# Half of the output products of both branches by seven instead of eight, with their operands made beside the gate units

## The chip, the cores and the metric

One core of a Trainium2 chip runs the kernel. The metric is device time in microseconds (us). The kernel before takes 2490.22 us, the median of three runs from 2490.2 to 2490.33.

## The reference, cut to what matters

Two layers (`DEPTH = 2`) act on 640 tokens of 1024 features: 512 frames of new streams and 8 x 16 frames of running ones. Each layer has a feed-forward half, a mixer, and a second feed-forward half. The change lies in the end of the mixer:

```
z  = h @ w_in            # conv B | conv C | conv V | q | k | v | gates
g  = sigmoid(g + b_gate); g_conv, g_attn = split(g)
m  = g_conv * (y_conv @ w_conv_out) + g_attn * (y_attn @ w_attn_out)
x += m @ w_o
```

`y_conv` and `y_attn` have 512 features each; `g_conv`, `g_attn` and `m` have 1024. All of it is float32.

## The kernel before, in words

**Layout.** Features lie on the 128 partitions and the 640 tokens along the free dimension, so 1024 features are eight tiles of 128 x 640. The tokens are cut into halves t1 and t2 of 320. All weights come as one stream `in_wst` of 512 KB pieces (`raw`, three buffers), in the order in which they are used. The function `_stream` lays them out, following `mixer_order`.

**Precision.** A float32 value is split into a high part of type fp32r and a low part, the rest: ScalarE casts `whi<-raw` (L347) and VectorE subtracts `wlo<-raw,whi` (L352). A product is three matmuls: high by high, high by low, low by high. Operands are split in the same way (L234 and L235).

**Slabs.** The weights in their two parts are called a slab here: `whi` and `wlo` of 128 x 1024, three buffers each. `slab()` takes the next slab and prepares the one two places on; `prep` issues the cast, `flush` the subtraction, `ahead` the sums of weights that the next slab needs.

**Products by seven.** Where two tiles of outputs (or of features) and two halves of tokens form a 2 x 2 problem, seven half products take the place of eight, at the price of sums of weights and of operands. The seven kinds of operands are called X11, X21, XN6, XT5, XT7, X22 and XT4. Their weights take two pieces of the stream and make four slabs: the first is piece one as it is; the second needs three sums of 128 x 512 on VectorE (L287, `raw<-raw,raw`, `s<-raw,raw` and a second `raw`), the third needs one more (`raw<-s,raw`), the fourth (half a slab) none. `gate_pair` in `outputs` does one pair of gate tiles so: seven blocks of 12 matmuls of 320 columns (L442), in three PSUM banks `qa`, `qb`, `qc`. Blocks X11 and X21 use the first slab, XN6 and XT5 the second, XT7 and X22 the third, XT4 the fourth. Block XT7 ends in a VectorE sum `g<-qa,c` that has to be done before XT4 may add to the same bank. After the seven blocks VectorE has scaled both gates by the norm (L1495, L1503, L1509), and ScalarE takes the sigmoids (L1330).

**Products as they are.** `out(m, y)` multiplies one 128-column tile of `w_conv_out` or `w_attn_out` ("co" and "ao") by the four tiles of `y_conv` or `y_attn`: 4 x 3 x 2 = 24 matmuls of 320 columns (L418, PSUM tile `py`). VectorE multiplies `py` by the gate (L1526; for "ao" L1528 and a sum into `mm`). Two calls of `out` use one slab.

**Order of the stage.** `outputs` runs gates 2 and 3, then `out` 0 to 3, and from there a gate unit of two gates and two calls of `out` in turn, to gates 14 and 15 and `out` 14 and 15. Gates below 8 belong to the convolution branch, the others to attention. Inside gate unit 2 the four tiles of `y_conv` are split (`take`), inside unit 8 those of `y_attn`. During the last two `out` the sums `mm` are split for `w_o` (`give`), which follows with 8 x 48 matmuls.

**What sets the order.** In `outputs` TensorE, VectorE and ScalarE work strictly in the order in which the code issues instructions (`tc.manual_schedule(engines=ORDERED)`). An instruction that waits holds up everything behind it on its engine.

The lines that set the pace of a gate unit before:

```python
s3 = slab(True)[0]
DVE.tensor_tensor(out=u, in0=u, in1=rr, op=ALU.mult)
sigmoid(u, m)
...
block(pa, s3, 0, XT4, every, False, True)
DVE.tensor_tensor(out=g[:, t1], in0=pa, in1=rr[:, t1], op=ALU.mult)
sigmoid(g, m + 1, -1.0)
flush()
```

Of the kernel before, what the change touches and what calls it, by code (L numbers as in the profile page):

```python
# [55 lines left out]
)  # L56

ROWS = (1, 2)

MARGIN = 2, 4  # L60
LEAN = {"a0": (1, 6), "b0": (1, 5), "a1": (1, 5), "b1": (1, 5)}
# [52 lines left out]
def mixer_order():  # L114

    mix = lambda *rows: ("mix", rows)
    out = [("v", None)] + [mix(("q", p), ("k", p)) for p in range(AW // P)]
    for c in range(0, CT, 2):  # L120
        out += [mix(("C", c + i), ("V", c + i)) for i in range(2)] + [mix(("B", c), ("B", c + 1))]
    gates = [mix(("g", m), ("g", m + 1)) for m in range(0, 2 * KT, 2)]
    out += gates[:2] + [("co", m) for m in range(4)]
    for i, g in enumerate(gates[2:]):
        name, m = ("co", 4 + 2 * i) if i < 2 else ("ao", 2 * i - 4)
        out += [g, (name, m), (name, m + 1)]
    return out + [("o", m) for m in range(KT)]


def kinds():  # L130
# [5 lines left out]
def stages():  # L136

    out, done = [], []

    def end(kind):  # L140
        done.append((kind, out[:]))
        out.clear()

    def plain(n):
        out.extend([8] * (n // 8) + [n % 8] * (n % 8 > 0))

    def ffn(name):
        held = 0
        for what, a in ffn_order(name):
            if what == "gu":  # L150
                plain(held)
                held = 0
                out.append("gu")
            elif what == "std":
                held += 2 * KT
            elif what == "cut":
                plain(held)
                held = 0
            elif what == "rows":
                plain(held)  # L160
                held = 0
                out.append("gu")
            elif what == "ends":
                held += KT * len(a)
            else:
                held += sum(len(js) for _, js in a)
        plain(held)

    for l in range(L):
        ffn(f"a{l}")  # L170
        end("ffn")
        held = 0
        for what, _ in mixer_order():
            if what == "mix":
# [12 lines left out]
def two(ps):  # L187
    return ps[:, :, :HT]
# [7 lines left out]
def trunk(ctx: ExitStack, tc: tile.TileContext, xin, wst, small, pbias, samplebias, kcache, vcache, gfin,  # L196
# [137 lines left out]
    def prep(i):  # L334

        if i < len(ready) or i >= len(slabs):
            return
        assert i == len(ready)
        parts = source(i)
        hi = wp.tile([P, CH], F32R, tag="whi", name=f"whi{i}", bufs=3)  # L340
        lo = wp.tile([P, CH], F32R, tag="wlo", name=f"wlo{i}", bufs=3)
        ready.append((hi, lo))
        o = 0
        for src, c in parts:
            d = slice(o, o + c.stop - c.start)
            o = d.stop
            ACT.copy(hi[:, d], src[:, c])  # L347
            pending.append((lo[:, d], src[:, c], hi[:, d]))

    def flush():  # L350
        for lo, src, hi in pending:
            DVE.tensor_tensor(out=lo, in0=src, in1=hi.bitcast(F32), op=ALU.subtract)  # L352
        pending.clear()
# [82 lines left out]
    def block(ps, s, half, ops, ks, start, stop):  # L436

        for kp in ks:
            w = [z[:, (half * NP + kp) * P : (half * NP + kp + 1) * P] for z in s]
            xh, xl = ops(kp)  # L440
            for j, (a, b) in enumerate(((w[0], xh), (w[0], xl), (w[1], xh))):
                PE.matmul(ps, a, b, start=start and kp == 0 and j == 0,  # L442
                          stop=stop and kp == NP - 1 and j == 2, skip_group_check=True)
# [869 lines left out]
    def mixer(l, after):  # L1313
        with tc.tile_pool(name=f"yp{l}", bufs=1, reuse_waits="tile") as yp, \
# [84 lines left out]
            with tc.tile_pool(name=f"gp{l}", bufs=1, reuse_waits="tile") as gp, \  # L1399
                 tc.manual_schedule(engines=ORDERED):  # L1400
                hold[0] = True
                mo = outputs(l, gp, ops.X, st, cs, ycs, yas, sigmoid, gates)
        ex = after()
        with tc.manual_schedule(engines=ORDERED):
            hold[0] = True
# [56 lines left out]
        def t5(self, kp):  # L1462
            self.parts(*(z[:, HT:] for z in self.h[2 * kp]), self.a[kp][:, 1])

    def outputs(l, gp, X, st, cs, ycs, yas, sigmoid, gates):
# [4 lines left out]
        mm = ycs + [spare[i // 2][:, i % 2] for i in range(CT)]  # L1470
        X11, X21, X22, XN6, XT5, XT7, XT4 = (X[i] for i in ("11", "21", "22", "N6", "T5", "T7", "T4"))
        c1, u2, c5 = cs
        every = range(NP)

        def gate_pair(m, then=None):
            n = f"{l}_{m}"
            pa, pb, pc = (att(f"q{i}{n}")[:, :HT] for i in "abc")
            u, g = gates[m], gates[m + 1] = tmp(f"g{n}"), tmp(f"g{n}_1")
            s0 = quiet()
            block(pa, s0, 0, X11, every, True, True)  # L1480
            ACT.copy(c1, pa)
# [9 lines left out]
            ACT.copy(c5, pc)  # L1491
            s2 = slab(True)[0]
            block(pa, s2, 0, XT7, every, False, True)
            add(g[:, t2], pa, c5)
            DVE.tensor_tensor(out=g[:, t2], in0=g[:, t2], in1=rr[:, t2], op=ALU.mult)  # L1495
# [7 lines left out]
            DVE.tensor_tensor(out=u, in0=u, in1=rr, op=ALU.mult)  # L1503
# [5 lines left out]
            DVE.tensor_tensor(out=g[:, t1], in0=pa, in1=rr[:, t1], op=ALU.mult)  # L1509
            sigmoid(g, m + 1, -1.0)  # L1510
            flush()

        def parts(pool, tag, name, src):
            hi, lo = (pool.tile([P, T], F32R, tag=f"{tag}{i}", name=f"{name}{i}") for i in ("hi", "lo"))
            split(hi, lo, src)
            return hi, lo

        def out(m, y, then=None):

            py = acc(f"py{l}_{m}")  # L1520
            product(py, y)
            if then:
                then()
            g = gates[m]
            if m < KT:
                DVE.tensor_tensor(out=halves(mm[m]), in0=two(py), in1=halves(g), op=ALU.mult)  # L1526
# [5 lines left out]
        yc, ya, mo = [], [], []  # L1532

        def take(y, name, srcs):
# [7 lines left out]
        gate_pair(2, lambda: take(yc, "yc", ycs))  # L1542
        for m in range(4):
            out(m, yc)
        for m in range(4, 2 * KT, 2):
            gate_pair(m, (lambda: take(ya, "ya", [yas[:, c, :] for c in range(CT)])) if m == KT else None)
            y = yc if m < KT else ya
            last = m == 2 * KT - 2
            out(m, y, (lambda: give(range(3))) if last else None)
            out(m + 1, y, (lambda: give(range(3, 6))) if last else None)  # L1550
        give(range(6, KT))
        return mo

# [518 lines left out]
def _stream(i):  # L2072
# [9 lines left out]
    for l in range(L):  # L2082
# [36 lines left out]
        for what, m in mixer_order():  # L2119
            if what == "v":  # L2120
                out.append(v.reshape(KT // 2, 2, P, AW).transpose(0, 2, 1, 3).reshape(-1, P, CH))
            elif what == "mix":
                out.append(chunks(held))
                held = []

                out.append(chunks([rows[name][a][o::2] for name, a in m for o in range(2)]))
            else:
                held.append(rows[what][m])
        out.append(chunks(held))
# [71 lines left out]
```

## Time and profile before

| | |
|---|---|
| median of three runs | 2490.22 us |
| the profiled execution, its own time | 2489.97 us |
| its span, first to last instruction | 2488.2 us |
| TensorE busy, matmuls | 2473.6 us (99%), 17312 matmuls |
| VectorE busy | 2140.2 us (86%) |
| ScalarE busy | 1355.6 us (54%) |
| the stage `outputs`, layer 0 | about 635 to 778 us of the span |
| the same stage, layer 1 | about 1867 to 2010 us of the span |

How to read it: the busy time of an engine is the union of its instructions, so a share of 99% says that the engine has hardly a gap. Matmuls overlap: each is listed with about 309 ns, but the next one starts earlier. The start times in a timeline tell the pace. VectorE's instructions overlap a little as well.

### The profile page before, as it was taken

What the parts mean: (1) busy time and instruction counts of PE and PEld (TensorE: products, weight loads), DVE (VectorE), ACT (ScalarE), POOL (GpSimd) and SP (SyncE); (2) the same over time, 40 slices, a digit from 0 to 9 for tenths busy, and PEclk for the clock granted to TensorE, in tenths of its full rate; (3) what the DMA queues carried; (4) which work ended last, traced back from release to release, by engine and by line L of the source; (5) the groups of instructions that cost most, each with busy time, mean ns of one, the idle gap of its engine ahead of it and who ended that gap; (6) DMA issues with size and microseconds to landing.
All of it is one profiled execution on the core that took longest, in us unless ns stands there. A gap on an engine that the chain in (4) does not pass through costs nothing.

```text
span 2488.2 us, 43913 instructions
## 1 busy us (share of the span) xinstructions
PE 2473.6 (99%) x17312; PEld 2421.3 (97%) x17312; DVE 2140.2 (86%) x3533; ACT 1355.6 (54%) x2151; POOL 295.2 (12%) x449
## 2 busy tenths in 40 slices
PE   9999999999999999999999999999999999999998
PEld 8999999889999999999999999998999999999998
DVE  7999998888777899998799999988886769999997
ACT  6555556665444555555665555566644455555555
POOL 0111112211000001111001011121110000111111
PEclk9999999999999999999999999999999999999999
DMA  4443544335223334445334343453442233444444
GB/s 155 126 118 101 125 117 123 113 106 174 77 85 111 94 102 106 112 117 120 99 92 111 109 117 102 116 128 107 133 157 86 77 111 88 109 115 106 112 117 117
DMA packets 109710, 279.22 MB, mean 112 GB/s; under 512 B 12448, under 2 KB 52000, under 8 KB 109504
## 3 DMA queue, kind: packets, MB, share of 16 engines
q1 hardware_dynamic: 69552, 220.10, 28.2%
q0 software_dynamic: 39520, 56.08, 12.2%
q8 instruction: 135, 2.21, 0.4%
q14 instruction: 71, 0.58, 0.1%
q10 hardware_dynamic: 432, 0.25, 0.0%
HBM read 230.56 MB, written 7.94 MB: 96 GB/s over the span
## 4 chain that ended last, share of the span: by engine, by line
PE 92%; DVE 4%; ACT 2%; issue 1%; DMA 1%; SPq 0%; DVEq 0%; ACTq 0%; POOLq 0%
PE pab L442 12%; PE paa L442 11%; PE pcb L442 6%; PE daa L1120 6%; PE pca L442 5%; PE dab L1120 5%; PE py L418 4%; PE po L418 4%; PE qa L442 4%; PE pbb L442 3%; PE dca L1120 3%; PE pba L442 3%; PE dcb L1120 2%; PE ma_cv L442 2%; PE ma_qk L442 2%; PE pv L1607 2%
## 5 line engine op out<-in xcount | busy, mean ns | idle before, releaser
L352 DVE TENSOR_TENSOR wlo<-raw,whi 128x1024 fp32r<-128x1024 f32 (+1 forms) x569 | 580.0, 1021 | 156.2 <-ACT whi L347 151.8
L347 ACT CAST whi<-raw 128x1024 fp32r<-128x1024 f32 (+1 forms) x569 | 505.2, 891 | 381.8 <-PE pbb L442 47.3
L347 ACT CAST whi<-s 128x1024 fp32r<-128x1024 f32 (+1 forms) x158 | 150.4, 952 | 296.1 <-issue 111.3
L442 PE MATMUL pab<-xhib,whi 128*128 128x320 f32 x704 | 217.7, 309 | 0.0
L442 PE MATMUL pab<-xhib,wlo 128*128 128x320 f32 x704 | 217.3, 309 | 0.0
L442 PE MATMUL pab<-xlob,whi 128*128 128x320 f32 x704 | 217.2, 309 | 0.0
L442 PE MATMUL paa<-xloa,whi 128*128 128x320 f32 x640 | 197.6, 309 | 0.6 <-DVE xloa L679 0.6
L442 PE MATMUL paa<-xhia,whi 128*128 128x320 f32 x640 | 197.9, 309 | 0.2 <-DVE ga L287 0.2
L442 PE MATMUL paa<-xhia,wlo 128*128 128x320 f32 x640 | 197.6, 309 | 0.0
L352 DVE TENSOR_TENSOR wlo<-s,whi 128x1024 fp32r<-128x1024 f32 (+1 forms) x158 | 173.4, 1098 | 4.4 <-ACT whi L347 4.4
L1142 POOL DMA_DIRECT2D x<-c_a x80 | 69.9, 1021 | 574.9 <-ACT ahia L1024 205.6
L442 PEld LDWEIGHTS pab<-xhib,whi 128*128 128x128 f32 x704 | 132.1, 188 | 0.9 <-issue 0.9
L442 PEld LDWEIGHTS pab<-xlob,whi 128*128 128x128 f32 x704 | 132.2, 188 | 0.0
L442 PEld LDWEIGHTS pab<-xhib,wlo 128*128 128x128 f32 x704 | 132.2, 188 | 0.0
L1142 POOL DMA_DIRECT2D x<-c_b x72 | 62.7, 1001 | 582.2 <-ACT ahib L1024 205.8
L442 PEld LDWEIGHTS paa<-xhia,whi 128*128 128x128 f32 x640 | 120.1, 188 | 1.3 <-DVE ga L287 0.5
L442 PEld LDWEIGHTS paa<-xloa,whi 128*128 128x128 f32 x640 | 120.2, 188 | 1.1 <-DVE xloa L679 1.1
L442 PEld LDWEIGHTS paa<-xhia,wlo 128*128 128x128 f32 x640 | 120.2, 188 | 0.2
L442 PE MATMUL pcb<-xhib,wlo 128*128 128x320 f32 x352 | 108.8, 309 | 0.0
L442 PE MATMUL pcb<-xlob,whi 128*128 128x320 f32 x352 | 108.6, 309 | 0.0
L442 PE MATMUL pcb<-xhib,whi 128*128 128x320 f32 x352 | 108.6, 309 | 0.0
L287 DVE TENSOR_TENSOR raw<-s,raw 128x512 f32<-128x512 f32 x158 | 107.9, 683 | 0.0
(757 smaller groups left out, 8072.4 us busy)
## 6 DMA issues: line engine op xcount, KB each, us to landing
raw<-in_wst SPq DMA_DIRECT2D x375, 512.0 KB, 3.6
x<-c_a POOLq DMA_DIRECT2D x80, 160.0 KB, 4.6
x<-c_b POOLq DMA_DIRECT2D x72, 160.0 KB, 3.6
lent<-in_wst POOLq DMA_DIRECT2D x34, 256.0 KB, 3.9
kc<-in_kcache SPq DMA_DIRECT2D x32, 256.0 KB, 4.8
vc<-in_vcache SPq DMA_DIRECT2D x16, 512.0 KB, 4.7
x<-u_a POOLq DMA_DIRECT2D x40, 160.0 KB, 4.0
x<-u_b POOLq DMA_DIRECT2D x36, 160.0 KB, 4.0
```

The costliest lines, as they stand in the source:

```text
L287: DVE.tensor_tensor(out=out, in0=a, in1=b, op=op)
L347: ACT.copy(hi[:, d], src[:, c])
L352: DVE.tensor_tensor(out=lo, in0=src, in1=hi.bitcast(F32), op=ALU.subtract)
L418: PE.matmul(ps[:, a, :HT], w, x[a] if isinstance(x, tuple) else x[:, a * HT : (a + 1) * HT], start=first and j == 0 and not seeded, stop=l ...
L442: PE.matmul(ps, a, b, start=start and kp == 0 and j == 0, stop=stop and kp == NP - 1 and j == 2, skip_group_check=True)
L1120: PE.matmul(ps[u], w, y, start=start and i == 0 and j == 0, stop=i == 1 and j == 2, skip_group_check=True)
L1142: POOL.dma_start(x[ms[2 * u + r]][:, cols], z[:, u], accum_op=ALU.add)
L1607: PE.matmul(pv[t], xx[:, t * P : (t + 1) * P], w[:, kk * AW : (kk + 1) * AW], start=c == 0 and kk == 0 and j == 0, stop=c == KT // 2 - 1 a ...
```

## The change

- **Seven for eight.** Output tiles 4 to 7 of the convolution branch and 2 to 5 of the attention branch no longer go through `out`. A new unit `rows` makes four tiles together: seven blocks of 12 matmuls of 320 columns, in PSUM tiles A, B (of the pool of `py`) and two banks `rc` (of the pool of `qa`). The weights of the four tiles come in the layout for seven products and make four slabs with four sums, as those of a gate unit do.
- **Operands.** XT5, XT7, XT4 and XN6 of `y` are made in place from each pair of its tiles (`mixed`): four VectorE instructions of 320 columns, a ScalarE cast of 1280 columns and a VectorE subtraction of 1280 columns. The three steps stand at three places of a gate unit: behind the first slab's flush, behind the copy of block XT5, and behind `ahead` of block XT7. Gate units 4, 6, 10 and 12 each carry one pair. X11, X21 and X22 are parts of the tiles that `take` split already.
- **Order.** Gates 2, `out` 0 to 3, gates 4, gates 6, `rows` of "co", gates 8, `out` 8 and 9, gates 10, gates 12, `rows` of "ao", gates 14, `out` 14 and 15. The products of `rows` "ao" are multiplied into the gates and added to `mm` in gate unit 14 (`total`).
- **Sigmoids.** They are collected in `lates` and issued behind the next unit's first ScalarE copy, or at the head of the next `out`.
- **Buffers.** The first four tiles of `mm` lie in new memory, the last four where `y_conv` lay.

The core of the diff:

```diff
+SEVEN = {"co": (4, 5, 6, 7), "ao": (2, 3, 4, 5)}
...
-        def gate_pair(m, then=None):
+        def gate_pair(m, at):
...
             ACT.copy(c1, pa)
+            due()
             prep(used[0] + 1)
             flush()
+            at[0]()
             block(pb, s0, 1, X21, every, True, True)
...
             ACT.copy(c5, pc)
+            at[1]()
             s2 = slab(True)[0]
...
             flush()
             ahead()
-            if then:
-                then()
+            at[2]()
             block(pc, s2, 1, X22, every, False, True)
...
-            sigmoid(u, m)
+            lates.append(lambda: sigmoid(u, m))
...
-            sigmoid(g, m + 1, -1.0)
+            lates.append(lambda: sigmoid(g, m + 1, -1.0))
...
+        def mixed(z):
+            z = z.rearrange("p c (a b) -> p (c a) b", a=2)
+            e1, e2, o1, o2 = (z[:, i] for i in range(4))
+            add(e1, e1, e2, ALU.subtract)
+            add(e2, o2, e2, ALU.subtract)
+            for out, a in ((o2, e1), (o1, o2)):
+                DVE.scalar_tensor_tensor(out=out, in0=a, scalar=-1.0, in1=out, op0=ALU.mult, op1=ALU.subtract)
+            yield
+            i = len(more) % 2
+            hi, lo = (gp.tile([P, 4, HT], F32R, tag=f"x{i}{p}", name=f"x{p}{l}_{len(more)}") for p in ("hi", "lo"))
+            ACT.copy(hi, z)
+            more.append((hi, lo))
+            yield
+            DVE.tensor_tensor(out=lo, in0=z, in1=hi.bitcast(F32), op=ALU.subtract)
+            yield
...
+            w = quiet()
+            mul(a, w, 0, X11, True)
+            ACT.copy(s1, two(A))
+            due()
+            prep(used[0] + 1)
+            flush()
+            mul(b, w, 1, X21, True)
+            add(s1, two(B), s1)
+            w = slab(True)[0]
+            flush()
+            mul(a, w, 0, XN6, False)
+            ACT.copy(s2, two(A))
+            gated(0, [s1[:, u] for u in range(2)], t1)
+            mul(c, w, 1, XT5, True)
+            for u in range(2):
+                ACT.copy(s5[:, u], c[u])
+            w = slab(True)[0]
+            mul(a, w, 0, XT7, False)
+            add(s5, two(A), s5)
+            flush()
+            ahead()
+            gated(1, [s5[:, u] for u in range(2)], t2, -1.0)
+            mul(c, w, 1, X22, False)
+            for u in range(2):
+                add(s2[:, u], c[u], s2[:, u])
+            w = slab(True)[0]
+            gated(0, [s2[:, u] for u in range(2)], t2)
+            mul(a, w, 0, XT4, False)
+            flush()
+            gated(1, a, t1, -1.0)
...
+        beside(4, ycp[0])
+        beside(6, ycp[1])
+        rows("co", yc)
+        gate_pair(8, [none, none, lambda: take(ya, "ya", [yas[:, c, :] for c in range(CT)])])
+        out(8, ya)
+        out(9, ya)
+        beside(10, yas[:, 0:2])
+        beside(12, yas[:, 2:4])
+        rows("ao", ya)
+        gate_pair(14, [lambda: total(0), none, lambda: (total(1), give(range(1)))])
+        out(14, ya, lambda: give(range(1, 4)))
+        out(15, ya, lambda: give(range(4, 6)))
```

`gated` multiplies a staged sum or a PSUM tile by two gates, 320 columns at a time; `beside(m, z)` is gate unit m with the three steps of `mixed(z)`.

More of the change, by code (lines that the diff above doesn't have):

```diff
@@ L122, in mixer_order @@
     gates = [mix(("g", m), ("g", m + 1)) for m in range(0, 2 * KT, 2)]
[L123 to L127, printed above, removed]
+    out += gates[:2] + [("co", m) for m in range(4)] + gates[2:4] + [("rows", ("co", SEVEN["co"]))]
+    out += [gates[4], ("ao", 0), ("ao", 1), gates[5], gates[6], ("rows", ("ao", SEVEN["ao"]))]
+    return out + [gates[7], ("ao", 6), ("ao", 7)] + [("o", m) for m in range(KT)]
 def kinds():
@@ L173, in stages @@
         for what, _ in mixer_order():
-            if what == "mix":
+            if what in ("mix", "rows"):
                 plain(held)
@@ L1401, in mixer @@
                 hold[0] = True
-                mo = outputs(l, gp, ops.X, st, cs, ycs, yas, sigmoid, gates)
+                mo = outputs(l, gp, ops.X, st, cs, ycp, yas, sigmoid, gates)
         ex = after()
@@ L1463, in t5, with outputs @@
             self.parts(*(z[:, HT:] for z in self.h[2 * kp]), self.a[kp][:, 1])
-    def outputs(l, gp, X, st, cs, ycs, yas, sigmoid, gates):
+    def outputs(l, gp, X, st, cs, ycp, yas, sigmoid, gates):
         rr, t1, t2 = st.rr, slice(0, HT), slice(HT, T)
         spare = [gp.tile([P, 2, T], F32, name=f"mm{l}_{i}") for i in range(2)]
-        mm = ycs + [spare[i // 2][:, i % 2] for i in range(CT)]
+        ycs = [z[:, i] for z in ycp for i in range(2)]
+        mm = [spare[i // 2][:, i % 2] for i in range(CT)] + ycs
+        stage = [halves(st.caps)] + [gp.tile([P, 2, HT], F32, name=f"rs{l}_{i}") for i in range(2)]
         X11, X21, X22, XN6, XT5, XT7, XT4 = (X[i] for i in ("11", "21", "22", "N6", "T5", "T7", "T4"))
@@ L1473, in outputs, with due @@
         every = range(NP)
-        def gate_pair(m, then=None):
+        lates = []
+        def due():
+            for f in lates:
+                f()
+            lates.clear()
+        def gate_pair(m, at):
             n = f"{l}_{m}"
@@ L1532, in outputs @@
         yc, ya, mo = [], [], []
+        more = []
         def take(y, name, srcs):
@@ L1540, in give @@
                 mo.append(parts(hp, "h", f"m{l}_{m}", mm[m]))
-        gate_pair(2, lambda: take(yc, "yc", ycs))
+        def mixed(z):
[13 more added lines that the diff above has]
+            yield
@@ L1543, in outputs, with total, beside @@
+        def total(r):
+            for m in SEVEN["ao"][2 * r : 2 * r + 2]:
+                add(mm[m], mm[m], gates[KT + m])
+        def beside(m, z):
+            z = mixed(z)
+            gate_pair(m, [lambda: next(z)] * 3)
+        none = lambda: None
+        gate_pair(2, [none, none, lambda: take(yc, "yc", ycs)])
         for m in range(4):
             out(m, yc)
[L1545 to L1550, printed above, removed]
+        beside(4, ycp[0])
@@ L2126, in _stream @@
                 out.append(chunks([rows[name][a][o::2] for name, a in m for o in range(2)]))
+            elif what == "rows":
+                out.append(chunks(held))
+                held = []
+                name, ms = m
+                out.append(chunks([rows[name][a][o::2] for r in range(2) for o in range(2)
+                                   for a in ms[2 * r : 2 * r + 2]]))
             else:
```

33 lines of the change are left out of this document (added).

## Prediction

> **What bounds the kernel now.** I read the page first, then the waits of TensorE, the chain that ended last, and then one gate unit instruction by instruction on VectorE and ScalarE.
>
> ```profile
> span 2488.2 us, 43913 instructions
> PE 2473.6 (99%) x17312; PEld 2421.3 (97%) x17312; DVE 2140.2 (86%) x3533; ACT 1355.6 (54%) x2151; POOL 295.2 (12%) x449
> ...
> PE poa L418 <- ACT whi L735: 5.4, 1, 5.4
> PE paa L442 <- DVE xloa L679: 0.6, 1, 0.6
> PE po L418 <- DVE m_6lo L235: 0.4, 2, 0.2
> ...
> 674.17 7.04 PE py L418 x48
> 693.51 7.04 PE py L418 x48
> ```
>
> TensorE is the bound. It waits 5.4 us once, at the start, and its other waits are below 1 us each. So a matmul less is time saved, and every wait that TensorE gets is time lost. The last two rows give the pace: 48 matmuls of two calls of `out` take 7.04 us, 0.1467 us each. Between them lie 693.51 - 674.17 - 7.04 = 12.30 us, one gate unit of 84 matmuls. One block of 12 takes 1.76 us. VectorE at 86% is next; whether it can follow is the question.
>
> ```profile
> 681.99 0.68 DVE L287 TENSOR_TENSOR raw<-s,raw 128x512 f32<-128x512 f32 x1
> 684.41 1.22 DVE L352 TENSOR_TENSOR wlo<-raw,whi 128x1024 fp32r<-128x1024 f32 x1 [1.75 <-ACT whi L347]
> 685.56 0.48 DVE L287 TENSOR_TENSOR g<-qb,capsm 128x320 f32<-128x320 f32 x1
> 685.96 0.68 DVE L352 TENSOR_TENSOR wlo<-raw,whi 128x512 fp32r<-128x512 f32 x1
> 690.10 0.49 DVE L287 TENSOR_TENSOR g<-qa,c 128x320 f32<-128x320 f32 x1 [3.46 <-PE qa L442]
> 690.63 0.49 DVE L1495 TENSOR_TENSOR g<-g,rrm 128x320 f32<-128x320 f32 x1
> 691.04 1.22 DVE L352 TENSOR_TENSOR wlo<-raw,whi 128x1024 fp32r<-128x1024 f32 x1
> 692.17 0.48 DVE L287 TENSOR_TENSOR g<-qc,capsm 128x320 f32<-128x320 f32 x1
> 692.69 0.83 DVE L1503 TENSOR_TENSOR g<-g,rrm 128x640 f32<-128x640 f32 x1
> 693.55 0.49 DVE L1509 TENSOR_TENSOR g<-qa,rrm 128x320 f32<-128x320 f32 x1
> 693.95 1.22 DVE L352 TENSOR_TENSOR wlo<-raw,whi 128x1024 fp32r<-128x1024 f32 x1
> 695.20 0.69 DVE L287 TENSOR_TENSOR raw<-raw,raw 128x512 f32<-128x512 f32 x1
> 695.93 0.69 DVE L287 TENSOR_TENSOR s<-raw,raw 128x512 f32<-128x512 f32 x1
> 696.54 0.69 DVE L287 TENSOR_TENSOR raw<-raw 128x512 f32<-128x512 f32 x1
> 697.14 0.82 DVE L1526 TENSOR_TENSOR mm<-py,g 128x640 f32<-128x640 f32 x1
> 697.88 0.68 DVE L352 TENSOR_TENSOR wlo<-s,whi 128x512 fp32r<-128x512 f32 x1
> ...
> 683.00 0.43 ACT L1481 COPY capsm<-qa 128x320 f32<-128x320 f32 x1 [4.46 <-PE qa L442]
> 683.32 1.06 ACT L347 CAST whi<-raw 128x1024 fp32r<-128x1024 f32 x1
> 684.67 0.62 ACT L347 CAST whi<-raw 128x512 fp32r<-128x512 f32 x1 [0.29 <-PE qb L442]
> 688.27 0.43 ACT L1491 COPY c<-qc 128x320 f32<-128x320 f32 x1 [1.33 <-PE qc L442]
> 693.55 1.55 ACT L1330 ACTIVATE g<-g,sm 128x640 f32<-128x640 f32 x2 [0.86 <-DVE g L1503]
> ...
> 681.04 0.31 PE L442 MATMUL qa<-hhim,whi 128*128 128x320 f32 x1
> ```
>
> This is gate unit 6, which starts at 681.04. In the first column the starts of neighbours give what VectorE really spends on one instruction: 0.40 us for 320 columns (685.56 to 685.96), 0.60 for 512 (697.88 to its other half), 0.74 for 640 (697.14 to 697.88), 1.14 for 1024 (684.41 to 685.56), so 1.40 for 1280 by the same slope. One that needs the result of the one before starts 0.13 later (690.10 to 690.63 is 0.53; 695.20 to 695.93 is 0.73). VectorE idles 1.75 and 3.46 us here: in a gate unit it has room. But note where: it waits for block XT7 (690.10 is 9.05 us into the unit), and nearly all its work comes after that. The sums for the next unit (695.20 on) fall under the calls of `out`, with 7.04 us for them.
>
> **What the change takes from TensorE.** A group of four tiles falls from 4 x 24 = 96 matmuls to 84. There are two groups in a layer and two layers: 48 matmuls x 0.1467 = **7.04 us less**. The columns are 320 as before and `rows` has the blocks of a gate unit, so I keep the pace.
>
> **What it adds to VectorE and ScalarE.** Of the built program I read the order on each engine, which is fixed in this stage. A gate unit costs VectorE: slabs 1.14 + 1.20 + 1.14 + 0.60, sums 4 x 0.60 + 0.12, gates 5 x 0.40 + 0.74 + 2 x 0.13; together 9.6 us. A step of `mixed` adds 4 x 0.40 + 3 x 0.13 = 2.0 and a subtraction of 1.40: **13.0 us against 12.32 us of TensorE**. The scalar_tensor_tensor in it costs as much as a plain one:
>
> ```profile
> L1079 DVE SCALAR_TENSOR_TENSOR doa<-doa 128x320 f32<-128x320 f32 x18 | 8.7, 484 | 0.0
> raw<-in_wst SPq DMA_DIRECT2D x375, 512.0 KB, 3.6
> ```
>
> `rows` costs 6.6 for slabs and their sums, 2 x 0.74 for the sums over two tiles, 10 x 0.40 + 0.13 for the rest: 12.2 us. So gates 4, gates 6 and `rows` ask 38.2 us of VectorE in 36.96 us of TensorE, with no `out` between them. ScalarE gets a cast of 1280 columns, 1.25 us by the slope of its rows; with slabs 3.6, three copies 1.2 and sigmoids 1.55 it is at 7.6 of 12.3 us, and only its place in the chains counts.
>
> **The walk.** Time 0 is the start of gate unit 4; VectorE has caught up there, as in the rows (681.99 comes 0.95 us into the unit).
> - *Gates 4.* The third slab is split at 3.36 to 4.58, as before. `mixed` runs 4.50 to 6.5, the sum on `qb` and the fourth slab end at 7.5. All this fits before XT7 (9.05). After it: 9.05 sum, 9.58 scale, 9.98 next slab, 11.12 three weight sums, 13.05 subtraction of 1280, 14.45 sum on `qc`, 14.98, 15.72, and at 16.12 the first half of the second slab of gates 6, done at 16.80. TensorE needs it in gates 6 at 12.32 + 3.52 + 0.30 = 16.14: **0.7 us lost**.
> - *Gates 6.* The sum for the third slab ends at 18.0, behind all that; ScalarE has the two sigmoids done at 17.4, casts to 19.1, VectorE subtracts to 20.34, just in time for 20.38. That idle 1.2 us of VectorE is not made good: `mixed` to 22.3, then 0.4 and 0.6. The sum on XT7 ends at 23.75, where XT4 could start at 23.60: **0.15 lost**. The cast of 1280 (price 1.25) stands before the cast of the next slab, which ends at 24.6. The chain of gates 4 from there gives the second slab of `rows` at 31.44; TensorE needs it at 29.4: **2.1 lost**.
> - *`rows`.* Third slab at 34.99 for 35.0. Two sums, eight products and the next weight sums: second slab of gates 8 at 44.1 for 43.8, the third at 48.4 for 47.65: **0.3 + 0.8 lost** in gates 8. That unit has no step of `mixed`, but the split of `y_attn` (4 x 0.74), so VectorE ends it 1.2 us later than in gate unit 2 or 4 before, and `out` 8 and 9 make good most of it.
> - *Gates 10, 12, `rows` "ao", gates 14.* The same, but VectorE comes about 1.2 us late: **2.1** in gates 12, **2.1** in `rows`, **1.1** in gates 14. There four sums of `total` are added (3.0 us) and a split; VectorE ends `out` 15 late, and the split of tile 6 for `w_o` is late by some 0.9 where it was 0.2: **0.7 lost**.
>
> Sum for a layer: 0.85 + 2.1 + 1.1 + 2.1 + 2.1 + 1.1 + 0.7 = 10.1 us; two layers 20.2. The edits with no price: the moved sigmoids lie in ScalarE's room, and where the price of a sigmoid (0.78) enters, it is in the walk; the stream has as many pieces, and a piece lands in 3.6 us where the walk leaves about 5 in gate units and 4 in `rows`; `rows` uses PSUM banks that are free by then. Without that cover a late piece costs up to 1 us for each `rows`. I bound the lost time from 2 (VectorE only late once per group, with the buffers taking up the rest) to 28 us (each wait a third longer, and late pieces).
>
> Profiled execution 2489.97 - 7.04 + 20.2 = 2503.1. Its median of runs lies 0.25 higher: **2503.4 us**, rounded 2503.5.
>
> **The rivals.**
> 1. *VectorE is late only by its surplus work.* The three slab buffers let it shift work between units, so only the surplus counts: 38.2 - 37.0 = 1.2 us a group and the 0.7 us chain behind XT7, four groups: 8 us lost, 2491. For it: nearly all waits of TensorE are below 1 us now at 86%. Against: order is fixed, and the preparation of a slab starts only when TensorE takes the slab two before it.
> 2. *The buffers hide it all*: 2490.2 - 7.0 = 2483.2, **faster**. The mechanism is the chain from the end of XT7 to the second slab of the next unit. TensorE leaves 7.34 us for it (four blocks and two matmuls). It decides at that point: I make the chain 8.05 us with the 1.40 us subtraction in it, and 6.6 without. If the subtraction overlapped more than the rows of 512 and 1024 show, the chain would fit.
> 3. *The waits cost TensorE its clock as well.* After the idle start, matmuls come at half pace:
>
> ```profile
> 8.99 0.47 PE L418 MATMUL poa<-xhia,whi 128*128 128x320 f32 x1
> 9.26 0.47 PE L418 MATMUL poa<-x2hia,whi 128*128 128x320 f32 x1
> ...
> 9.96 0.31 PE L418 MATMUL poa<-xhia,wlo 128*128 128x320 f32 x1
> 10.11 0.31 PE L418 MATMUL poa<-x2hia,wlo 128*128 128x320 f32 x1
> ```
>
> They start 0.27 us apart at 8.99 and 0.15 apart from 9.96 on, after a few us of work. If each of the six waits of 2.1 us set this off for some 3 us, 1.5 us each would be lost: 2503 + 9 = 2512. Against: what set it off there was an idle time of over 5 us. [...]
>
> [...]
>
> **How the numbers follow.** Forecast (the walk, waits of 14 to 28 us in all, 2497 to 2511): 0.64. Rival 1 (2486 to 2496): 0.20. Rival 2 (2483): 0.07. Rival 3, with late pieces in some cases (2511 to 2517): 0.09. A measurement of this kernel tells about 0.2% from no change, 5 us: faster means below 2485.2, slower above 2495.2. Faster 0.07; same 0.17 (most of rival 1); slower 0.76. The range 2489 to 2512 leaves out rival 2, a part of rival 1 and the upper end.
>
> **What would show it.** TensorE 48 matmuls fewer. In the waits of TensorE, `wlo` from VectorE (L352) on `qa` and on the PSUM tile A of `rows`, 1 to 2 us each, at the second slab of gates 6, 12 and both `rows`; about 10 us a layer, and VectorE without idle time over 30 us there. Gate unit 4 itself without a wait. Wrong would be: no such waits (rival 2), waits at the first slabs or for pieces of the stream, or matmuls 0.27 us apart inside the stage.

## The result, and the profile after

The changed kernel takes 2512.66 us (median of 4 runs, 2512.46 to 2512.76), the kernel before beside it 2490.27 (4 runs, 2490.2 to 2490.52): a ratio of 1.009, with a 95% interval of 1.0077 to 1.0103. It is 22.4 us slower, 9.2 us above the forecast of 2503.5 and 0.7 us above the upper end of the range. The profiled execution took 2512.46 us by its own time.

The first lines of the page of the changed kernel:

```profile
span 2510.7 us, 43957 instructions
...
PE 2478.9 (99%) x17264; PEld 2419.9 (96%) x17264; DVE 2192.9 (87%) x3633; ACT 1378.6 (55%) x2187; POOL 295.6 (12%) x449
```

TensorE does 17312 - 17264 = 48 matmuls less, as foreseen, and VectorE is busy 53 us more. So 7.04 us were saved and 22.4 + 7.0 = 29.4 us lost elsewhere. The waits of TensorE in the changed kernel say where (who waits, for whom: us in total, times, longest):

```profile
PE poa L418 <- ACT whi L735: 5.6, 1, 5.6
PE qa L442 <- DVE wlo L352: 5.3, 4, 1.9
PE po L418 <- DVE g L1540: 4.0, 2, 2.0
PE raco L1597 <- ACT capsm L1612: 2.3, 2, 1.2
PE raao L1597 <- ACT capsm L1612: 2.3, 2, 1.2
PE qa L442 <- ACT capsm L1500: 1.9, 4, 0.5
PE raao L1597 <- DVE wlo L352: 1.0, 2, 0.5
PE raco L1597 <- DVE wlo L352: 1.0, 2, 0.5
```

The first is the wait at the start, as before. The other seven are new, and all lie in `outputs` or at its end. Two of the names are of ScalarE copies. Both copies stand behind work of VectorE: that in `rows` (L1612) waits for a sum (e3), and that in gates 8 and 14 (L1500) stands on ScalarE behind the casts of two slabs, of which the first waits for VectorE's sum of weights (gates 8, layer 0):

```profile
709.72 1.57 ACT L347 CAST whi<-raw 128x1024 fp32r<-128x1024 f32 x2 [3.48 <-DVE raw L287]
711.19 0.42 ACT L1500 COPY capsm<-qa 128x320 f32<-128x320 f32 x1
```

The seven add to 17.8 us, less than 29.4, for two reasons. This view counts from the modelled end of the last matmul, 0.2 to 0.3 us after the next could have started. And it doesn't see a TensorE that works at half pace. Both are seen in the starts of the weight loads. Gates 6 and `rows` "co" of layer 0, changed kernel (start, duration, in brackets the idle time before and who ended it):

```profile
677.68 0.19 PEld L442 LDWEIGHTS qa<-tlo,whi 128*128 128x128 f32 x1
678.85 0.19 PEld L442 LDWEIGHTS qa<-thi,wlo 128*128 128x128 f32 x1 [0.98 <-DVE wlo L352]
...
691.03 0.19 PEld L1597 LDWEIGHTS rbco<-yc_3hi,wlo 128*128 128x128 f32 x1
692.65 0.19 PEld L1597 LDWEIGHTS raco<-xhi,whi 128*128 128x128 f32 x1 [1.43 <-ACT capsm L1612]
692.76 0.19 PEld L1597 LDWEIGHTS raco<-xlo,whi 128*128 128x128 f32 x1
693.71 0.19 PEld L1597 LDWEIGHTS raco<-xhi,wlo 128*128 128x128 f32 x1 [0.76 <-DVE wlo L352]
...
694.24 0.33 PEld L1597 LDWEIGHTS raco<-xhi,wlo 128*128 128x128 f32 x1
694.50 0.33 PEld L1597 LDWEIGHTS raco<-xhi,whi 128*128 128x128 f32 x1
```

Loads normally start 0.147 us apart; 677.68 to 678.85 is 1.17. In `rows` one wait follows another, with two matmuls between them, and from 694 on the loads come 0.26 us apart. The stretches around it (us; busy and count of TensorE, weight loads, VectorE, ScalarE, GpSimd; granted clock; DMA share; GB/s):

```profile
690.00:694.00 4.00, 2.34 (x15) 1.81 (x14) 3.96 (x6) 2.65 (x5) 0.00 (x0) 0.99 0.00 0
694.00:697.20 3.20, 3.20 (x14) 3.20 (x14) 2.09 (x4) 2.40 (x4) 0.00 (x0) 0.50 0.00 0
697.20:700.00 2.80, 2.80 (x20) 2.80 (x20) 2.13 (x4) 1.76 (x4) 0.00 (x0) 0.97 0.66 196
```

For 3.2 us the granted clock is 0.50, right after the waits: 13 loads that take 0.26 us each, 1.5 us lost. There are three such stretches in this execution (693.7, 789.6 and 2001.3 us), 4.4 us in all.

Taken unit by unit from the starts of the loads, against 0.1467 us each and without the half-clock stretches, a layer loses: gates 6 1.2, `rows` "co" 2.3, gates 8 1.0, gates 12 2.45, `rows` "ao" 2.4, gates 14 1.0, before `w_o` 2.3, and 0.1 in gates 10: 12.75 us. Twice that and 4.4 us are 29.9, against the 29.4 to be explained.

### The profile page after: what moved, and what is told of

Its sections match the earlier page's. It is cut to its first block, busy times and chain, and to the rows that moved or that the text cites. A ratio compares the mean times of both kernels' runs of the same rounds, so it can differ in the third digit from the quotient of the medians.

```text
span 2510.7 us, 43957 instructions
## 1 busy us (share of the span) xinstructions
PE 2478.9 (99%) x17264; PEld 2419.9 (96%) x17264; DVE 2192.9 (87%) x3633; ACT 1378.6 (55%) x2187; POOL 295.6 (12%) x449
## 4 chain that ended last, share of the span: by engine, by line
PE 86%; DVE 9%; ACT 2%; issue 2%; DMA 1%; SPq 0%; DVEq 0%; ACTq 0%; POOLq 0%
PE pab L442 12%; PE paa L442 11%; PE pcb L442 6%; PE daa L1120 6%; PE pca L442 5%; PE dab L1120 5%; PE po L418 5%; PE pbb L442 3%; PE dca L1120 3%; PE pba L442 3%; DVE wlo L352 3%; PE dcb L1120 2%; PE ma_cv L442 2%; PE ma_qk L442 2%; PE pv L1721 2%
## 5 line engine op out<-in xcount | busy, mean ns | idle before, releaser
L352 DVE TENSOR_TENSOR wlo<-raw,whi 128x1024 fp32r<-128x1024 f32 (+1 forms) x577 | 585.9, 1018 | 158.1 <-ACT whi L347 154.7
```

## The experiments

The first theory was the queue: VectorE, in its fixed order, is late where units with four slabs follow each other, and half clock behind the waits comes on top. The first four kernels try its parts: the order of units, the wait before `w_o`, the ScalarE copy in `rows`, and the place of the sigmoids. The rival for each is that its part has no share.

**e1_spread: two calls of `out` between the units** (the stream of weights follows the new order).

```diff
-        for m in range(4):
-            out(m, yc)
+        out(0, yc)
+        out(1, yc)
         beside(4, ycp[0])
+        out(2, yc)
+        out(3, yc)
         beside(6, ycp[1])
```

> The changed kernel with one thing moved: the convolution branch runs gates 2, out 0, out 1, gates 4, out 2, out 3, gates 6, rows (the changed kernel has all four calls of out ahead of gates 4). Same work, same instructions. Theory 'VectorE comes late where units with four slabs follow each other' (queue): the wait in gates 6 (1.2 us a layer) goes, that of rows of co falls from 2.4 to about 1.0, gates 8 loses nothing (1.0 before), gates 12 about 1.2 instead of 2.4: some 9 us, and one stretch at half clock (1.5 us) less: about 2502. Rival 'the amount of work decides' (VectorE has the same sum of work in the stage): no change, 2512.

Measured: 2504.12 us (2503.23 to 2504.68), a ratio of 1.0056 (1.0039 to 1.0073): 8.5 us of the 22.4 come back with no instruction removed; 1.5 of them are clock, as the profiled execution has two half-clock stretches in place of three. The loss in gates 6 is gone, and that in `rows` "co" falls from 2.3 to 1.2. But gates 8 still loses 1.0 and gates 12 2.2, where I had expected 0 and 1.2:

```profile
PE qa L442 <- DVE wlo L352: 3.9, 2, 1.9
```

These two are the waits in gates 12. Their lateness isn't inherited from the units of the other branch, as I had it. At block XT7 of gates 8 VectorE waits for TensorE:

```profile
709.96 0.49 DVE L287 TENSOR_TENSOR g<-qa,c 128x320 f32<-128x320 f32 x1 [0.90 <-PE qa L442]
```

So the lateness arises behind it, where the split of `y_attn` stands, with one pair of `out` to make it good. That the total still came near the 2502 expected is in part luck: `rows` "ao", where nothing was moved, fell from 2.4 to 1.15 in both layers. There TensorE had run at half clock in gates 12 just before, losing 1.44 us in which VectorE could catch up. The profiled execution of e3 has both cases: with such a stretch in gates 12 (layer 0) `rows` "ao" loses 1.2, without one (layer 1) 2.3.

**e2_then: the splits for `w_o` behind the product with the gate.** The call of `then` in `out` moves behind the VectorE instructions that read `py`.

```diff
             product(py, y)
-            if then:
-                then()
             g = gates[m]
...
                 add(mm[m - KT], mm[m - KT], g)
+            if then:
+                then()
             flush()
```

> The changed kernel with one thing moved: in out 14 and out 15 the splits of finished tiles for w_o come behind the multiplication of py by the gate, not ahead of it. Theory 'the first product with w_o waits for the PSUM bank of py 14, which VectorE frees late because three splits stand in front': the wait of 2.25 us before that product falls to some 1.0 us on a later tile, in both layers: 2.5 us less, and up to 1.5 us more if the stretch at half clock behind it goes: 2508.5 to 2510. Rival 'the splits themselves are late, the bank is not what holds it': no change, 2512.5.

Measured: 2507.7 us (2506.79 to 2509.03), 1.007 (1.0055 to 1.0085). The wait `po <- DVE g L1540` of 4.0 us is replaced by

```profile
PE po L418 <- DVE m_4lo L235: 1.7, 2, 0.9
```

and two half-clock stretches are left. 2.3 us of waits and 1.5 us of clock are 3.8 of the 4.1 us between the two profiled executions. What held `w_o` back is seen in the changed kernel on VectorE and on TensorE:

```profile
785.44 0.83 DVE L235 TENSOR_TENSOR m_1lo<-mm,m_1hi 128x640 fp32r<-128x640 f32 x1 [1.65 <-ACT m_1hi L234]
786.18 0.82 DVE L235 TENSOR_TENSOR m_2lo<-mm,m_2hi 128x640 fp32r<-128x640 f32 x1
786.92 0.82 DVE L235 TENSOR_TENSOR m_3lo<-mm,m_3hi 128x640 fp32r<-128x640 f32 x1
787.65 0.82 DVE L1540 TENSOR_TENSOR g<-py,g 128x640 f32<-128x640 f32 x1
...
788.61 0.53 PE L418 MATMUL po<-m_0hi,whi 128*128 128x320 f32 x2 [2.02 <-DVE g L1540]
```

The operand of the first product, tile 0, has long been split. TensorE waits for the PSUM bank of `py` of `out` 14, and the instruction that frees it (L1540) stands behind three splits of 0.74 us.

**e3_stage: the ScalarE copy in `rows` into memory of its own.** In the changed kernel the copy `capsm<-raco` (L1612) writes where gates 6 still has a sum to read, and so it waits for VectorE.

```diff
-        stage = [halves(st.caps)] + [gp.tile([P, 2, HT], F32, name=f"rs{l}_{i}") for i in range(2)]
+        stage = [gp.tile([P, 2, HT], F32, name=f"rs{l}_{i}") for i in range(2)] + [halves(st.caps)]
```

> The changed kernel with the first staged sum of rows in memory of its own (and the last one in the memory that it had), so that its copy on ScalarE no longer waits for VectorE's sum on qc of the gate unit before. Theory 'queue': the wait of 1.43 us for that copy goes, but the wait for the second slab behind it grows from 0.76 to 2.2 us, since the slab is ready when it was: within 0.5 us of 2512.7, but for stretches at half clock. Rival 'the shared buffer is a cause of its own': 4 x 1.4 = 5.7 us less, 2507.

Measured: 2511.72 us (2510.96 to 2513.11), 1.0086 (1.0071 to 1.0101), not to be told from the changed kernel. The wait for the copy is gone and the one behind it has grown by as much:

```profile
PE raco L1597 <- DVE wlo L352: 3.7, 2, 1.9
```

Before it was 2.3 for the copy and 1.0 for `wlo`. The list names whom TensorE waited for last; what sets the time is the slab that VectorE makes ready late.

**e4_sigmoid: the sigmoids back in their own unit**, each right behind the VectorE scaling that feeds it, as before the change.

```diff
-            lates.append(lambda: sigmoid(u, m))
+            sigmoid(u, m)
...
-            lates.append(lambda: sigmoid(g, m + 1, -1.0))
+            sigmoid(g, m + 1, -1.0)
```

> The changed kernel with the sigmoids issued where the kernel before issues them, inside their own gate unit. Theory 'queue': at the four places in a layer where no out follows the gate unit, the next unit's first copy stands behind sigmoids that wait for VectorE's last two products, and TensorE needs that copy for the third block: each of these waits grows by 1 to 1.3 us, 8 to 10 us in all, 2521 to 2523. Rival 'the sigmoids' place is free, since the weight slab is later anyway': no change, 2512.5.

Measured: 2522.62 us (2521.44 to 2524.11), 1.013 (1.0115 to 1.0145). Moving the sigmoids is worth 10 us to the changed kernel. The number was hit by luck, however: the waits of gates 6 and 12 grow by some 1.0 us each and those of `rows` by less than 0.5, under 5 us over both layers. The rest is clock: the profiled execution, at a mean of 0.994, has seven half-clock stretches with 11.4 us, where the changed kernel has three with 4.4. The largest of its waits is

```profile
PE qa L442 <- ACT capsm L1490: 10.0, 4, 3.1
```

A sigmoid that waits for a late VectorE holds up the next unit's first copy on ScalarE, and XN6 may not add to that bank until it is copied.

The next two test the price on VectorE and the clock.

**e5_pool: the operands made by GpSimd.** Five GpSimd instructions of 320 columns take the place of VectorE's four, and the subtraction of 1280 columns goes there too.

```diff
-            add(e1, e1, e2, ALU.subtract)
+            POOL.tensor_tensor(out=e1, in0=e1, in1=e2, op=ALU.subtract)
...
-            DVE.tensor_tensor(out=lo, in0=z, in1=hi.bitcast(F32), op=ALU.subtract)
+            POOL.tensor_tensor(out=lo, in0=z, in1=hi.bitcast(F32), op=ALU.subtract)
```

> The changed kernel with the making of the operands (all of mixed but the cast on ScalarE) on GpSimd, which is idle in this stage: five instructions of 320 columns and the subtraction of 1280 a step. VectorE has 9.6 instead of 13.0 us to do in gates 4, 6, 10 and 12; all else stays. Theory 'queue': the waits in gates 6 and 12 and in both rows go (8.5 us a layer, 17 in all) and the stretches at half clock behind them; those of gates 8, gates 14 and before w_o stay: 2491 to 2494. Rival 'more matrix work in a row is what TensorE waits for, or GpSimd is too slow or slows VectorE down': waits stay or move to rows, 2500 or more.

Measured: 2514.42 us (2514.12 to 2514.94), 1.0097 (1.008 to 1.0114): no gain, a miss by 20 us. GpSimd has the time, but a VectorE product that runs beside its subtraction takes longer (e5_pool, GpSimd's and VectorE's rows in order):

```profile
671.96 2.95 POOL L1570 TENSOR_TENSOR xlo<-yc,xhi 128x1280 fp32r<-128x1280 f32 x1 [9.94 <-ACT xhi L1567]
...
672.12 0.49 DVE L287 TENSOR_TENSOR g<-qa,c 128x320 f32<-128x320 f32 x1 [3.47 <-PE qa L442]
672.65 2.61 DVE L1507 TENSOR_TENSOR g<-g,rrm 128x320 f32<-128x320 f32 x1
675.18 1.21 DVE L352 TENSOR_TENSOR wlo<-raw,whi 128x1024 fp32r<-128x1024 f32 x1
```

The sum with one input in PSUM (`qa`) takes 0.49 us as ever. The product with both inputs in SBUF takes 2.61 us instead of 0.49, and ends 0.35 us after GpSimd's subtraction. The work was taken off VectorE's queue, and the time was not: VectorE is busy 2194.8 us with 40 instructions fewer, against 2192.9. In the row above the price is 2.1 us; over the 14 products of this line in the run the duration goes from 0.49 to 2.61 us, with a median of 1.41. Whether the place of the inputs decides it was not shown.

**e6_fill: matmuls that do nothing useful, put into the waits.** 8 before block XN6 of `rows` and 12 before `w_o`, into PSUM that is free: 2 x (2 x 8 + 12) = 56 matmuls more.

```diff
+            for _ in range(8):
+                PE.matmul(c[1], w[0][:, :P], y[0][0][:, t1], start=True, stop=True, skip_group_check=True)
             add(s1, two(B), s1)
...
+                    for _ in range(12):
+                        PE.matmul(idle, mo[0][0][:, :P], mo[0][0][:, :HT], start=True, stop=True, skip_group_check=True)
```

> The changed kernel with TensorE kept at work in its long waits: eight matmuls of 320 columns with no use in front of the third block of rows (1.17 us, where it waits 1.43 us) and twelve in front of the first product with w_o (1.76 us, where it waits 2.25 us). Theory 'clock': the three stretches at half pace (1.5 us each) come from the waits, so they go and the time falls by 3 to 4.6 us although TensorE does more: 2508 to 2509.7. Rival 'half pace does not come from the waits': no change, 2512.7; if the waits were not waits for other engines, 5.9 us more.

Measured: 2508.66 us (2508.07 to 2509.19), 1.0074 (1.0059 to 1.0089), 4.0 us faster with 56 matmuls more. Its clock, and the same stretches of `rows` as above:

```profile
core 0: 2507.2 us, clock 1.000
```

```profile
690.00:694.00 4.00, 3.93 (x26) 3.41 (x24) 3.96 (x7) 2.44 (x4) 0.00 (x0) 1.00 0.00 0
694.00:697.20 3.20, 2.78 (x19) 2.78 (x20) 2.09 (x4) 2.55 (x5) 0.00 (x0) 1.00 0.00 0
```

Where the clock was 0.50 it is 1.00, VectorE's work in these stretches being the same. The fill can make no useful matmul ready earlier; what it took away are the half-clock stretches. So 4 of the 22.4 us are the clock.

Then came versions meant to keep the saving.

**e7_behind: the subtraction of 1280 moved to the next unit**, behind that unit's first flush, so that it isn't in the chain behind XT7.

```diff
             prep(used[0] + 1)
+            for z in behind:
+                next(z)
+            behind.clear()
             flush()
...
-            gate_pair(m, [lambda: next(z)] * 3)
+            gate_pair(m, [lambda: next(z)] * 2 + [none])
+            behind.append(z)
```

> The changed kernel with one step moved: the subtraction of 1280 columns (third step of mixed) no longer stands behind block XT7 of its gate unit but in the next unit, where VectorE idles about 1.2 us between the sum for the third slab and the ScalarE cast of it. No work less. Theory 'queue' (the prediction's point of decision: the chain behind XT7 is 8.05 us with the subtraction and 6.6 without, against 7.34): the wait in gates 6 goes (1.0 us), those of rows fall from 2.2 to some 0.4, gates 12 from 2.2 to 0.8; gates 8, gates 14 and w_o stay: 12 us less and some 3 us of half clock, 2496 to 2501. Rival 'the sum of work on VectorE (13.0 against 12.3 us a unit) decides': it is unchanged, so at most 3 us less, 2509 or more.

Measured: 2512.19 us (2507.52 to 2513.04), 1.0084 (1.007 to 1.0098), a miss by more than 11 us. The wait in gates 6 is gone and that in gates 12 falls from 2.2 to 0.8, as expected. But the subtraction of the second pair now falls into `rows`, whose own XN6 block needs it:

```profile
PE raco L1601 <- DVE xlo L1573: 4.1, 2, 2.0
PE raao L1601 <- DVE xlo L1573: 4.1, 2, 2.0
```

I had followed the slabs through the queue and not the operand that I was moving. One of the four runs took 2507.52 us at a mean clock of 0.999, the other three 2512.16 to 2513.04 at 0.996 to 0.997; the profiled execution, one of the three, lost 5.5 us to half clock.

**e8_all: the order of e1, the places of e2 and e7 (all five splits in `out` 14), and the last four products of `rows` put off to the next unit.** The last is new:

```diff
-            gated(0, [s2[:, u] for u in range(2)], t2)
             mul(a, w, 0, XT4, False)
             flush()
-            gated(1, a, t1, -1.0)
+            def rest():
+                gated(0, [s2[:, u] for u in range(2)], t2)
+                gated(1, a, t1, -1.0)
+            return rest
```

> All that helped together: the calls of out spread (e1), the subtraction in the next unit (e7), the splits for w_o behind the multiplication of py 14 (e2, with all five in out 14), and the last four of the eight products of rows put behind the next gate unit's third slab, so that gates 8 and 14 do not wait for it. TensorE has 48 matmuls fewer than the kernel before, as in the changed kernel. Theory 'queue': some 1 to 2 us of waits a layer are left, no half clock: 2490.2 - 7.0 + 2 to 4 = 2485 to 2487. Rival 'seven for eight does not pay at this load of VectorE': 2490 or more.

Measured: 2500.12 us (2499.99 to 2501.76), 1.0043 (1.0029 to 1.0056), a miss by 13 us. The loss in gates 8 is gone, which neither e1 nor e7 took away, so putting off the products works; the waits of `rows` for `xlo` (3.2 and 4.1 us) stay, as in e7.

**e9_co: only the convolution branch by seven**, placed as in the changed kernel; attention goes through `out` as before.

```diff
-        beside(10, yas[:, 0:2])
-        beside(12, yas[:, 2:4])
-        rows("ao", ya)
+        for m in (10, 12):
+            gate_pair(m, [none] * 3)
+            out(m, ya)
+            out(m + 1, ya)
```

> One half of the change alone: the convolution branch as in the changed kernel, the attention branch as in the kernel before. TensorE has 24 matmuls (3.5 us) fewer than before. Theory 'queue': the waits of gates 6, rows of co and gates 8 stay (1.2 + 2.4 + 1.0 us a layer, 9.3 in all), with up to two stretches at half clock (0 to 3 us): 2496 to 2499. Rival 'the waits sit in the attention part': 2488.

Measured: 2495.9 us (9 runs, 2495.61 to 2497.26), 1.0024 (1.0014 to 1.0033). 24 matmuls saved (3.5 us), 5.7 us slower than the kernel before (2490.2 in these runs), 9.2 lost: gates 6 1.25, `rows` 2.5 and gates 8 1.0 are 4.75 a layer, 9.5 for two. So this branch alone has the losses that it has in the changed kernel. Its nine runs stand in two groups, 2495.6 to 2496.0 and 2497.2 to 2497.3; the step of 1.4 us fits one half-clock stretch, but only an execution of the lower group was profiled, and it has none.

**e10_co_spread: the same branch, placed otherwise.** Two calls of `out` between the units (e1), the last products of `rows` put off (e8), the cast behind the copy of XN6 and the subtraction ahead of the XT7 sum, where VectorE otherwise waits for TensorE.

```diff
             ACT.copy(u2, pa)
+            if early:
+                at[1]()
             block(pc, s1, 1, XT5, every, True, True)
...
             block(pa, s2, 0, XT7, every, False, True)
+            if early:
+                at[2]()
             add(g[:, t2], pa, c5)
```

> The convolution branch alone by seven, with the work put where VectorE idles: calls of out spread as in e1, the cast of the operands behind the copy of block XN6 and their subtraction ahead of the sum on XT7 (VectorE idles 1.5 us there), the last products of rows behind the next unit's third slab as in e8. The attention branch as in the kernel before. Theory 'queue': the chain behind XT7 is 6.6 us against 7.34, so no wait over 0.3 us is left in the stage, and 24 matmuls x 0.1467 = 3.5 us are saved whole: 2486.7 to 2487.5, below the kernel before. Rival 'the surplus of work always costs': 2490 or more.

Measured: 2487.43 us (11 runs, 2487.15 to 2487.77), the kernel before 2490.3 (19 runs, 2490.05 to 2490.76): a ratio of 0.9988 (0.998 to 0.9997), **faster than before**. Of the 3.5 us that 24 matmuls are worth, 2.9 arrive. VectorE's queue in gates 6, and gates 4 to the end of `rows` as one window (columns as above; the numbers of lines are one higher in e9 and e10):

```profile
682.56 1.49 DVE L1576 TENSOR_TENSOR xlo<-yc,xhi 128x1280 fp32r<-128x1280 f32 x1 [0.39 <-ACT xhi L1573]
683.97 0.48 DVE L288 TENSOR_TENSOR g<-qa,c 128x320 f32<-128x320 f32 x1
```

```profile
655.00:706.00 51.00, 50.97 (x347) 50.68 (x347) 43.66 (x67) 24.59 (x37) 0.00 (x0) 1.00 0.22 73
```

The same subtraction stands in front of `g<-qa,c`, the sum that waits for XT7, instead of behind it; it ends as that sum becomes possible, and TensorE is without a gap through gates 6 and `rows`. In gates 4 it waits once in each layer:

```profile
663.95 0.19 PEld L443 LDWEIGHTS qc<-hhim,whi 128*128 128x128 f32 x1 [0.29 <-ACT c L1505]
```

This load starts 0.33 us late, behind the copy of `qc`, which on ScalarE stands behind the early cast. Over two layers that is about the 0.6 us that doesn't arrive. No run separates the three parts of this placing.

**e11_both: both branches in this way**, with the splits for `w_o` placed as in e8; gates 12 keeps the old place for its subtraction.

```diff
-            gate_pair(m, [lambda: next(z)] * 3)
+            gate_pair(m, [lambda: next(z)] * 3, m != 12)
```

> Both branches by seven with the same placing (gates 12 alone keep the subtraction where the changed kernel has it), and the splits for w_o as in e8. Theory 'queue': the convolution branch has no waits; in the attention branch gates 10, 12 and rows follow the split of y_attn with one pair of out between, so some 0.5 in gates 12, 1.5 to 2 in rows, 0.7 in gates 14 and 1 before w_o stay, about 4 us a layer against 3.5 saved by a branch: 2489 to 2492. Rival 'spread work leaves no waits': 2484.

Measured: 2497.66 us (8 runs, 2496.07 to 2499.34), 1.0029 (1.0019 to 1.0039), a miss by more than 5 us. 3.6 us of the loss are a wait like that of e10's gates 4, but much longer. It is in gates 10; the rows of VectorE and ScalarE under it are of layer 0:

```profile
PE qc L442 <- ACT c L1504: 3.6, 2, 1.8
```

```profile
726.75 1.02 DVE L1568 SCALAR_TENSOR_TENSOR ya<-ya 128x320 f32<-128x320 f32 x2
...
727.80 1.26 ACT L1572 CAST xhi<-ya 128x1280 fp32r<-128x1280 f32 x1 [2.42 <-DVE ya L1568]
728.97 0.42 ACT L1504 COPY c<-qc 128x320 f32<-128x320 f32 x1
```

The early cast stands ahead of the copy of `qc` on ScalarE. In gates 6 VectorE has its operand ready in time, in gates 4 0.3 us late; in gates 10, behind the split of `y_attn`, it is late, the cast waits for it and the copy for the cast. The waits in `rows` "ao" (2.4 us), gates 14 (0.8) and before `w_o` (1.8) stay, with two half-clock stretches. I found no place in which the attention half pays. Whether there is one stays open.

## Why the prediction came out as it did

- **Right: the direction and the mechanism.** The saving is 7.04 us (e10 keeps 2.9 of 3.5 for half of it), and TensorE then waits for slabs that VectorE makes ready late. The prices were near. The four operand instructions took 1.98 us (2.0), and the subtraction of 1280 columns takes 1.41 (1.40), as the rows of gates 4 in the changed kernel show:

```profile
666.37 1.01 DVE L287 TENSOR_TENSOR yc<-yc 128x320 f32<-128x320 f32 x2
...
668.35 0.48 DVE L287 TENSOR_TENSOR g<-qb,capsm 128x320 f32<-128x320 f32 x1
...
675.05 1.48 DVE L1569 TENSOR_TENSOR xlo<-yc,xhi 128x1280 fp32r<-128x1280 f32 x1
676.46 0.48 DVE L287 TENSOR_TENSOR g<-qc,capsm 128x320 f32<-128x320 f32 x1
...
678.11 0.68 DVE L352 TENSOR_TENSOR wlo<-s,whi 128x512 fp32r<-128x512 f32 x1
```

  Six of the seven waits of a layer are where the walk put them, with their sizes to 0.35 us: gates 6 0.85 forecast and 1.2 measured, `rows` 2.1 and 2.3, gates 8 1.1 and 1.0, gates 12 2.1 and 2.45, `rows` "ao" 2.1 and 2.4, gates 14 1.1 and 1.0. Together 9.35 were forecast and 10.35 measured, 2.0 us too little over both layers.
- **Wrong: the term before `w_o`, 0.7 forecast and 2.3 measured.** "The split of tile 6 for `w_o` is late by some 0.9 where it was 0.2" follows the operands. TensorE waited for a PSUM bank instead, that of `py` 14 behind three splits (e2). This is 3.2 us over both layers.
- **Wrong: rival 3 left out of the sum.** It was priced correctly, 1.5 us for a wait, and given 0.09, as if the clock either took part in all six waits or in none. It took part in three of the eight long ones: 4.4 us, which e6 shows. The reason given against it, that the one known case came after more than 5 us idle, is a case and no bound. Here 1.43 and 0.76 us with two matmuls between them were followed by half clock. No run shown ahead of the result has the "some 3 us" that the price rests on: behind the idle start the loads came at half pace, 0.27 us apart, from 5.6 to 9.8 us. The changed kernel's stretches then lasted about 3.2 us. Why only three of eight waits of one size were followed by one, no run shows.
- The three together are 2.0 + 3.2 + 4.4 = 9.6 us; 9.2 lie between forecast and result.
- **Rivals 1 and 2 failed** for the reason given against the first: order. e1 changes nothing but the order of the units and gains 8.5 us. The decision point of rival 2 was right, and e7 shows it from the other side: with nothing but the 1.40 us subtraction out of the chain behind XT7, the wait in gates 6 is gone.
- **The signs.** Gates 4 has no wait, as said. Of the signs of being wrong one came, the matmuls 0.27 us apart inside the stage. "VectorE without idle time over 30 us" was wrong. The changed kernel from 671 to 706 us (columns as above):

```profile
671.00:706.00 35.00, 32.63 (x206) 31.49 (x205) 30.59 (x47) 17.08 (x26) 0.00 (x0) 0.95 0.23 73
```

  VectorE, though late, is busy 30.59 of 35 us. In each unit it stands idle for 1.1 to 1.2 us until ScalarE has cast the third slab, whose sum it made itself just before. Such holes were in the walk and forgotten in the sign.
- **The sigmoids**, costed at nothing, are worth 10 us to the changed kernel (e4): without the move, a late VectorE would also have stopped ScalarE's copies, for under 5 us of waits and the rest in half clock behind them. The surplus of VectorE was fixed; what it costs depends on what is queued behind it.

## What to carry to other kernels

Where engines run in a fixed order, a step's price is its place: the same operands cost the convolution branch 9.2 us of lost time where they were put, and 0.6 us in front of the sum that waits for TensorE, with calls of `out` between the units and the last products put off (e9, e10). Walk the queue for every resource that the next engine needs, operands and PSUM banks alike, and for the operand that you move. Add the clock to the waits in the sum, not as a case beside it: here three of eight waits of about 2.2 us on TensorE cost 1.5 us more each.

## What the runs showed of the hardware

- TensorE's clock fell to 0.50 for some 3 us after three of the eight waits of about 2.2 us in all of the changed kernel, 12 or 13 matmuls at 0.26 to 0.27 us. Nor does a longer wait decide it: in e4 the same wait of 3.4 us in gates 12 is followed by a granted clock of 1.00 in layer 0 and of 0.50, over the 3.20 us of the second row, in layer 1 (columns as in the stretches at the top):

```profile
746.10:750.00 3.90, 3.89 (x26) 3.90 (x27) 2.66 (x5) 2.07 (x4) 0.00 (x0) 1.00 0.05 14
1994.80:1998.00 3.20, 3.12 (x12) 3.12 (x13) 2.00 (x4) 1.59 (x3) 0.00 (x0) 0.50 0.02 5
```

  With matmuls without use in the waits the profiled execution kept a granted clock of 1.000 (e6).
- A GpSimd subtraction of 128 x 1280 fp32 took 2.95 us, one of 320 columns 1.2 to 1.85. While it ran, a VectorE product of 320 columns with both inputs in SBUF took 2.61 us in place of 0.49, and a sum with an input in PSUM still 0.49 (e5).
